# The second group's three fetched tiles: the scores go to DRAM, and their best 16 are searched in the dense pass

## The chip, the cores and the metric

The kernel runs on one core of one Trainium2 chip. The metric is the device time of one execution in microseconds. The engines are called PE (TensorE, matrix products), DVE (VectorE), ACT (ScalarE), POOL (GpSimd) and SP (SyncE, here only a queue of DMA issues). A line number such as L751 is a line of the kernel before.

## The reference, cut to what matters

One layer of a model: two mixers, then a channel mixer that looks up 16 of 16,384 single-neuron experts for each of 8 heads and each token. There are 9 tiles of 128 tokens. Of the channel mixer:

```python
def peer(x, w_q, sub_keys, u_tab, v_tab):
    q = (xt @ w_q).reshape(n_tok, PEER_HEADS, 2, PEER_QHALF)
    s = jnp.einsum('thpc,hpkc->thpk', q, sub_keys).astype(jnp.float32)
    v1, i1 = lax.top_k(s[:, :, 0], PEER_TOPK)
    v2, i2 = lax.top_k(s[:, :, 1], PEER_TOPK)
    cand = (v1[..., :, None] + v2[..., None, :]).reshape(n_tok, PEER_HEADS, PEER_TOPK * PEER_TOPK)
    ...
    top_v, top_j = lax.top_k(cand, PEER_TOPK)
    idx = jnp.take_along_axis(cand_idx, top_j, axis=-1)
    g = jax.nn.softmax(top_v, axis=-1)
    ...
        ue = jnp.take(u_tab, ib, axis=0)
        ve = jnp.take(v_tab, ib, axis=0)
        a = jax.nn.gelu(jnp.einsum('bd,bed->be', xb, ue)) * gb
        return jnp.einsum('be,bed->bd', a, ve)
```

So each token has 16 score vectors (8 heads, 2 halves) of 128 scores, and of each the best 16 values and their indices are needed. From these 32 the candidates of a head are formed, the best 16 of them chosen, and the experts' rows of two tables (1024 wide) used.

## The kernel before, in words

**Tiles and groups.** Tile 0 holds the context, tiles 1 to 8 the latent tokens. They pass through `group` as [0], then GA = [5,6,7,8], then GB = [1,2,3,4]. In the end the experts are computed in two ways. Tiles 0 to 3 (`GATHER`) are *fetched*: for each of 128 experts per token POOL fetches a row of 1024 with an indirect DMA (L802 from the first table, L815 from the second), DVE forms the dot product (L805) and, after the gelu, accumulates (L820); that is 256 row steps per tile. Tiles 5, 6, 7, 8 and 4 (`DENSE`) go through *all* experts, in a dense pass over 128 blocks e: a product with the first table (`hidden`, tile pH), the gelu (L988, tile a), DVE's multiplication with the weights in G (L1069), a split of the result in a high and a low half (ACT L99 for the high one, DVE L100 for the low one), and the product with the second table. Every matrix product here is made of three products of such halves (L129, L130, L131). The weights' tables are split in the same way as they arrive (uH/uL, vH/vL). Three of the five dense tiles keep their sums in PSUM (tile pout); the other two are "rotated": once in 4 blocks their products (tile prot) are added on DVE to accd (L1052).

**The query stage** of a group (end of `group`, from L738): 16 blocks b, each with a weight unit that is loaded and split (wH, wL), 24 matrix products into pq, a copy of them on ACT (qs, L748), the score products into one PSUM bank psc (one for each tile of the group, L751) and, for each tile, `top16` (L413 to L420) on DVE: MAX8, the index search, the replacement of the eight found, MAX8 and index search again. Values go to tv, indices to ti. For a dense tile `combine` follows (tile 4's in two halves, the first from block 8 on), with the indices turned into rt, and `build_G` forms G and writes it to DRAM (G_d), from where the dense pass reads it (tile Gt, L1061). For a fetched tile of GB, tv and ti are sent to DRAM (L760) and `combine` is left for later.

**The dense pass** does this later work: `combine_late` (L767) loads tv and ti of one tile (L780), runs `combine` in steps, and queues the tile's row steps. `fill`, called 16 times in 4 blocks (after each split and each rotated addition), issues 3 late steps for the first of the three tiles and 0.8 for the others (`LATE`), a later tile's from 60 row steps before the running tile's end (`LEAD`), and 1.525 row steps. While late work runs, the rows have the 4 buffers of one pool; otherwise 2 more, which are the ones that the late work uses. What late work issues on DVE passes through the helper `Paced`, so that the trace has it under one line, L119; row steps and late steps are held back by an order (not a wait) behind the last but one split.

All instructions' order on an engine is set by a scheduler from priorities and the data they need. SP issues nearly all loads and stores in program order of its own queue: a load that waits for its buffer holds back the ones behind it.

Of the kernel before, what the change touches and what calls it, by code (L numbers as in the profile page):

```python
# [9 lines left out]
F32 = mybir.dt.float32  # L10
# [10 lines left out]
NT = 9  # L21
# [30 lines left out]
def hybrid_kernel(ctx, tc, x_all, pos, c2t, w_ada, b_ada, wst, wspt, bsp, lbraw, vecs, fng, skt, state,  # L52
# [20 lines left out]
    o_d = dram.tile([NT, 128, 512], F32, name="o_d")  # L73
    tvi_d = dram.tile([NT, 128, 512], F32, name="tvi_d")
    h2r_d = dram.tile([NT, 128, D], F32, name="h2r_d")
# [486 lines left out]
    def group(gp, tiles, hpar, native):  # L562
# [164 lines left out]

        tv = [gp.tile([128, 8, 2, 16], F32, name="tv", bufs=n) for _ in range(n)]
        ti = [gp.tile([128, 8, 2, 16], U32, name="ti", bufs=n) for _ in range(n)]
        opd_q = lambda k: cut(h2, slice(None), k, slice(0, T))  # L730
        before = rate["gather"]
        rate["gather"] = before * RQ
        split_at = [i for i in range(n) if tiles is GB and tiles[i] in DENSE]
        halves = {}
        for b in range(16):
            if b == 8:
# [12 lines left out]
            pss = ptp("psc")  # L749
            for i in range(n):  # L750
                P.matmul(pss[:, i * 128:(i + 1) * 128], qs[:, i * 128:(i + 1) * 128], skb, start=True, stop=True)  # L751
            for i in range(n):
                top16(gp, pss[:, i * 128:(i + 1) * 128], tv[i][:, b // 2, b % 2, :], ti[i][:, b // 2, b % 2, :], 128)
        rate["gather"] = before
        for i in range(n):
            t = tiles[i]
            if tiles is GB and t in GATHER:

                for z, x in enumerate((tv[i], ti[i].bitcast(F32))):
                    nc.sync.dma_start(tvi_d[t][:, z * 256:(z + 1) * 256], x.rearrange("p a b c -> p (a b c)"))  # L760
                late.append(t)
            elif i in halves:
                choose_q.append(combine(gp, t, tv[i], ti[i], h0=4, res=halves[i]))
            else:
                choose_q.append(combine(gp, t, tv[i], ti[i]))

    def combine_late(t):  # L767
        cols = []

        def al(name, n, dt=F32):  # L770
            w = n if dt in (F32, U32) else (n + 1) // 2
            if not cols or cols[-1][1] + w > 1024:
# [6 lines left out]
        tvi = al("tvi", 512)  # L779
        nc.sync.dma_start(tvi, tvi_d[t])  # L780
        yield from combine(None, t, q(tvi[:, 0:256]), q(tvi[:, 256:512].bitcast(U32)), al,
                           lambda name: row(name).bitcast(F16), Paced())
# [223 lines left out]

    late_q = deque(combine_late(t) for t in late)
    C["coff"], C["clen"], C["cj"] = load_cs3(dp, row("cs32"))
# [185 lines left out]
```

## Time and profile before

| | us |
|---|---|
| median of 3 runs | 3658.97 (3655.87 to 3667.10) |
| the profiled execution | 3668.42 |
| its span in the trace | 3666.6 |
| query stage of GB (first to last score product) | 1558.69 to 1666.39 |
| first multiplication with G (the dense pass begins) | 1748.62 |
| late work of the second and of the third fetched tile begins | about 2237 and 2900 |
| last instruction on DVE | 3658.28 |

The profile's page shows PE busy in 91% of the span, DVE in 77%, ACT in 32% and POOL in 39%. In the dense pass a unit of four blocks takes 56.3 us where no late work runs (281.46 us for twenty blocks). An instruction's row in a timeline has start and duration in us, the engine, the line, the operation, out<-in; in brackets stands the idle time of its engine ahead of it and what ended it.

### The profile page before, as it was taken

To read this page: it belongs to the slowest core of one execution; us is meant where nothing else is said; L and a number is where in the kernel's file an instruction comes from. 1 tells how busy PE (TensorE), PEld (TensorE's weight loads), DVE (VectorE), ACT (ScalarE), POOL (GpSimd) and SP (SyncE) were. 2 spreads that over 40 slices of the span, in tenths; PEclk is the share of its full clock that TensorE was granted. 3 is DMA by queue.
4 is the path that set the end of the run, shared out by engine and by line. 5 is a ranking of instruction groups with operands and counts; after the bars stand their busy time and mean duration, and the time that the engine had idled before them with its cause. 6 is when DMAs were issued, how large, how long until landed. Compare 5 with 4: busy or idle time off the path is not lost. (4 is left out here: it accounts for less than half of the span.)

```text
span 3666.6 us, 48822 instructions
## 1 busy us (share of the span) xinstructions
PE 3343.5 (91%) x17547; PEld 2763.0 (75%) x17547; DVE 2841.6 (77%) x5427; ACT 1156.4 (32%) x2075; POOL 1436.9 (39%) x1128
## 2 busy tenths in 40 slices
PE   8888889898898899897899999989999989999997
PEld 4376778676576576576788888888898878898996
DVE  2317888787699986598787889887888888788888
ACT  2511334321323577726222222222222222222222
POOL 0002441454211220000265564655555456555654
PEclk9899999899999899897899999999999999999998
DMA  7787754688733676442898998898988799988986
GB/s 279 280 294 255 248 186 129 206 301 333 251 116 99 224 264 228 161 151 101 272 333 307 319 325 274 317 317 313 321 315 313 260 330 338 321 303 314 332 317 248
DMA packets 361956, 971.12 MB, mean 265 GB/s; under 512 B 32720, under 2 KB 142672, under 8 KB 356080
## 3 DMA queue, kind: packets, MB, share of 16 engines
q0 software_dynamic: 149824, 546.37, 42.3%
q1 hardware_dynamic: 211888, 421.62, 33.3%
q8 instruction: 138, 2.26, 0.2%
q14 instruction: 106, 0.87, 0.1%
HBM read 897.07 MB, written 70.80 MB: 264 GB/s over the span
## 5 line engine op out<-in xcount | busy, mean ns | idle before, releaser
L802 POOL DMA_INDIRECT gu<-in_urow_dram,ix x512 | 688.5, 1345 | 1003.7 <-DVE jk L805 374.1
L815 POOL DMA_INDIRECT gv<-in_vrow_dram,ix x512 | 694.9, 1357 | 736.4 <-DVE acc L820 399.9
L805 DVE SCALAR_TENSOR_TENSOR jk<-gu,h2r 128x1024 f16<-128x1024 f32 x512 | 625.6, 1222 | 139.9 <-DMA gu<-in_urow_dram,ix 124.8
L820 DVE SCALAR_TENSOR_TENSOR acc<-gv,act,acc 128x1024 f32<-128x1024 f32 x508 | 651.7, 1283 | 62.8 <-DMA gv<-in_vrow_dram,ix 53.3
L129 PE MATMUL pH<-h2DH,uH 128*128 128x320 f32 x2016 | 625.4, 310 | 12.9 <-DVE accd L1052 10.9
L131 PE MATMUL pH<-h2DH,uL 128*128 128x320 f32 x2016 | 622.9, 309 | 3.2 <-DVE uL L100 3.2
L130 PE MATMUL pH<-h2DL,uH 128*128 128x320 f32 x2016 | 623.4, 309 | 0.0
L129 PEld LDWEIGHTS pH<-h2DH,uH 128*128 128x128 f32 x2016 | 379.7, 188 | 23.0 <-DVE accd L1052 15.9
L130 PEld LDWEIGHTS pH<-h2DL,uH 128*128 128x128 f32 x2016 | 379.6, 188 | 4.4
L131 PEld LDWEIGHTS pH<-h2DH,uL 128*128 128x128 f32 x2016 | 379.4, 188 | 4.1 <-DVE uL L100 4.1
L129 PE MATMUL pout<-vH,aH 128*128 128x512 f32 x768 | 299.0, 394 | 23.0 <-ACT vH L99 16.3
L99 ACT ACTIVATE vH<-vr 128x1024 fp32r<-128x1024 f32 x128 | 133.4, 1058 | 568.9 <-DMA vr<-in_vrow_dram 294.3
L130 PE MATMUL pout<-vL,aH 128*128 128x512 f32 x768 | 302.0, 393 | 5.0 <-DVE vL L100 5.0
L131 PE MATMUL pout<-vH,aL 128*128 128x512 f32 x768 | 302.0, 393 | 2.1 <-DVE aL L100 2.1
L129 PE MATMUL prot<-vH,aH 128*128 128x512 f32 x512 | 211.7, 414 | 56.9 <-DVE accd L1052 50.8
L99 ACT ACTIVATE wH<-wraw 128x1024 fp32r<-128x1024 f32 x118 | 124.9, 1060 | 437.9 <-PE pq L130 145.2
L100 DVE TENSOR_TENSOR vL<-vr,vH 128x1024 fp32r<-128x1024 f32 x128 | 156.3, 1221 | 86.9 <-ACT vH L99 84.5
L130 PE MATMUL prot<-vL,aH 128*128 128x512 f32 x512 | 208.4, 407 | 0.0
L99 ACT ACTIVATE uH<-ur 128x1024 fp32r<-128x1024 f32 x126 | 133.3, 1058 | 237.1 <-PE pH L130 197.5
L131 PE MATMUL prot<-vH,aL 128*128 128x512 f32 x512 | 207.7, 406 | 0.0
L99 ACT ACTIVATE aH<-a 128x640 fp32r<-128x640 f32 x128 | 94.2, 736 | 357.1 <-DVE a L1069 284.2
L550 PEld LDWEIGHTS <-oh 128*128 128x128 f16 x1280 | 130.5, 120 | 80.7 <-issue 65.0
(343 smaller groups left out, 6442.7 us busy)
## 6 DMA issues: line engine op xcount, KB each, us to landing
wraw<-in_wst_dram SPq DMA_DIRECT2D x216, 512.0 KB
vr<-in_vrow_dram SPq DMA_DIRECT2D x128, 512.0 KB
ur<-in_ut_dram SPq DMA_DIRECT2D x126, 512.0 KB
G_d<-Gs SPq DMA_DIRECT2D x40, 1024.0 KB
Gt<-G_d SPq DMA_DIRECT2D x160, 256.0 KB
wraw<-in_w_ada_dram SPq DMA_DIRECT2D x48, 512.0 KB
gu<-in_urow_dram,ix POOLq DMA_INDIRECT x512
gv<-in_vrow_dram,ix POOLq DMA_INDIRECT x512
```

Of the source, the lines that this page charges most:

```text
L99: A.activation(H, src, AF.Copy)
L100: return V.tensor_tensor(out=L, in0=src, in1=H.bitcast(F32), op=OP.subtract)
L129: P.matmul(ps, a[0], b[0], start=first, stop=False)
L130: P.matmul(ps, a[0], b[1], start=False, stop=False)
L131: P.matmul(ps, a[1], b[0], start=False, stop=last)
L550: P.matmul(pg[:, tt * 128:(tt + 1) * 128], oh[:, 0, :, tt], og[a][:, :, tt], start=(a == 0), stop=(a == 1))
L802: G.indirect_dma_start(out=ur, out_offset=None, in_=urow, in_offset=bass.IndirectOffsetOnAxis(ap=ix[:, c:c + 1], axis=0))
L805: paced(V.scalar_tensor_tensor(jk, ur, 1.0, h2r, op0=OP.mult, op1=OP.mult, accum_out=dots[:, k:k + 1]))
L815: G.indirect_dma_start(out=vr, out_offset=None, in_=vrow, in_offset=bass.IndirectOffsetOnAxis(ap=ix[:, c:c + 1], axis=0))
L820: paced(V.scalar_tensor_tensor(acc, vr, act[:, k:k + 1], acc, op0=OP.mult, op1=OP.add))
```

## The change: what it does

In the query stage of GB only tile 4 is still searched. The scores of tiles 1 to 3 (384 columns of the PSUM bank) are copied by ACT into a buffer sw and sent by SP to DRAM (sc_d), once a block; the score product of tile 4 is put ahead of the other three. tv and ti no longer go to DRAM. In the dense pass `combine_late` loads a tile's scores in two loads of 512 KB into two row buffers (packets of 512 bytes) and searches them, 16 searches in 8 further steps, before the steps it had. From there on, nothing is changed; 12 lines are added, so that L1069 becomes L1081, L1061 becomes L1073, L805 becomes L817 and so on.

```diff
-    tvi_d = dram.tile([NT, 128, 512], F32, name="tvi_d")
+    sc_d = dram.tile([16, 128, 3 * 128], F32, name="sc_d")
...
+        wait = [i for i in range(n) if tiles is GB and tiles[i] in GATHER]
+        now = [i for i in range(n) if i not in wait]
...
             pss = ptp("psc")
-            for i in range(n):
+            for i in now + wait:
                 P.matmul(pss[:, i * 128:(i + 1) * 128], qs[:, i * 128:(i + 1) * 128], skb, start=True, stop=True)
-            for i in range(n):
+            if wait:
+                w0, m = wait[0], len(wait) * 128
+                sw = h512("sw")
+                A.activation(sw[:, :m], pss[:, w0 * 128:w0 * 128 + m], AF.Copy)
+                nc.sync.dma_start(sc_d[b], sw[:, :m])
+            for i in now:
                 top16(gp, pss[:, i * 128:(i + 1) * 128], tv[i][:, b // 2, b % 2, :], ti[i][:, b // 2, b % 2, :], 128)
...
-                for z, x in enumerate((tv[i], ti[i].bitcast(F32))):
-                    nc.sync.dma_start(tvi_d[t][:, z * 256:(z + 1) * 256], x.rearrange("p a b c -> p (a b c)"))
-                late.append(t)
+                late.append((t, wait.index(i)))
...
-        nc.sync.dma_start(tvi, tvi_d[t])
-        yield from combine(None, t, q(tvi[:, 0:256]), q(tvi[:, 256:512].bitcast(U32)), al,
+        tv, ti = q(tvi[:, 0:256]), q(tvi[:, 256:512].bitcast(U32))
+        for z in range(2):
+            sc = row("sc").rearrange("p (b j) -> p b j", b=8)
+            nc.sync.dma_start(sc, sc_d[z * 8:z * 8 + 8, :, w * 128:(w + 1) * 128].rearrange("b p j -> p b j"))
+            for b in range(8):
+                top16(None, sc[:, b, :], tv[:, z * 4 + b // 2, b % 2, :], ti[:, z * 4 + b // 2, b % 2, :], 128, Paced())
+                if b % 2:
+                    yield
+        yield from combine(None, t, tv, ti, al,
                            lambda name: row(name).bitcast(F16), Paced())
```

What this does to the order of instructions is seen at three places. **On DVE in the query stage**, a part of the searches that stand between two splits of weight units (wL) in a block before:

```order
L100 TENSOR_TENSOR wL<-wraw,wH 128x1024
L419 MAX tv<-mrep 128x8
L415 MAX tv<-psc 128x8
L420 MAX_INDEX ti<-tv,mrep 128x8
L416 MAX_INDEX ti<-tv,psc 128x8
L418 MATCH_REPLACE mrep<-tv,psc 128x128
L415 MAX tv<-psc 128x8
L419 MAX tv<-mrep 128x8
L416 MAX_INDEX ti<-tv,psc 128x8
L420 MAX_INDEX ti<-tv,mrep 128x8
L418 MATCH_REPLACE mrep<-tv,psc 128x128
```

and now the whole of what stands between two such splits:

```order
L100 TENSOR_TENSOR wL<-wraw,wH 128x1024
L415 MAX tv<-psc 128x8
L416 MAX_INDEX ti<-tv,psc 128x8
L418 MATCH_REPLACE mrep<-tv,psc 128x128
L419 MAX tv<-mrep 128x8
L420 MAX_INDEX ti<-tv,mrep 128x8
L100 TENSOR_TENSOR wL<-wraw,wH 128x1024
```

Four searches in a block have become one, and none of the three others is left in this stage.

**On DVE at the start of the dense pass**, from the last work on the G matrices (L533) over the cast of a table of constants (L873) to the first multiplications with Gt; before:

```order
L533 TENSOR_TENSOR oh<-oh,gl 128x512
L873 CAST cs_13760<-cs_13759 128x768
L1069 TENSOR_TENSOR a_13010<-a_13010,Gt 128x640
L1069 TENSOR_TENSOR a_13069<-a_13069,Gt 128x640
L119 TENSOR_TENSOR late<-late 128x8x16
L100 TENSOR_TENSOR aL<-a_13010,aH 128x640
```

and now (late is where the late work keeps its values, sc a tile's scores; the cast is L885, the multiplication L1081):

```order
L119 MAX_INDEX late<-late,sc 128x8 x2
L119 MATCH_REPLACE sc<-late,sc 128x128 x2
L119 MAX late<-sc 128x8 x2
L119 MAX_INDEX late<-late,sc 128x8 x2
L119 MAX late<-sc 128x8 x2
L119 MAX_INDEX late<-late,sc 128x8 x2
L119 MATCH_REPLACE sc<-late,sc 128x128 x2
L119 MAX late<-sc 128x8
L1081 TENSOR_TENSOR a_12758<-a_12758,Gt 128x640
L119 MAX_INDEX late<-late,sc 128x8
L119 MAX late<-sc 128x8
L1081 TENSOR_TENSOR a_12817<-a_12817,Gt 128x640
```

Between the cast and the first multiplication there stand now some five and a half searches of the first fetched tile, of which the piece shows the last rows (the first row of sc comes right behind the cast); the other ten and a half come behind the multiplication, between the splits of the first blocks.

**On SP's queue** where the second fetched tile's late work begins, with the loads of the dense pass around it (ur, vr: the two tables; Gt: the weights); before:

```order
L1061 DMA Gt<-G_d 128x4x128 x4
L1029 DMA vr<-in_vrow_dram 128x1024 [waits DMAHW3_49,DVE_49]
L780 DMA late<-tvi_d 128x512 [waits DMASW3_49,DMASW4_49,DMASW2_49,DMASW6_49,DMASW1_49,DMAHW4_49,DMASW0_49,DVE_49]
L1029 DMA ur<-in_ut_dram 128x1024 [waits DMAHW5_49,DVE_49]
L1029 DMA vr<-in_vrow_dram 128x1024 [waits DMAHW6_49,DMAHW3_49,DVE_49]
```

and now:

```order
L1041 DMA ur<-in_ut_dram 128x1024 [waits DMAHW7_49,DVE_49]
L1041 DMA vr<-in_vrow_dram 128x1024 [waits DMAHW6_49,DMAHW0_49,DVE_49]
L788 DMA sc<-sc_d 128x8x128 [waits DMASW3_49,DMASW4_49,DMASW2_49,DMASW6_49,DMASW1_49,DMAHW1_49,DMASW0_49,DVE_49]
L1041 DMA ur<-in_ut_dram 128x1024 [waits DMAHW2_49,DVE_49,Activation_49]
L788 DMA sc<-sc_d 128x8x128 [waits DMASW5_49,DMASW7_49,DMASW3_49,DMAHW3_49,DMASW1_49,DVE_49]
L1041 DMA vr<-in_vrow_dram 128x1024 [waits DMAHW4_49,DMAHW7_49,DVE_49,Activation_49]
```

The one load of 256 KB has become two of 512 KB with one load of ur between them, and each waits for its row buffer (the semaphores named DMASW are POOL's fetches, which used that buffer). The load of vr ahead of the first of them waits for DVE. On DVE itself the first search of these scores stands directly behind a split of ur, the one that sets this vr's buffer free:

```order
L100 TENSOR_TENSOR aL<-a,aH 128x640
L832 SCALAR_TENSOR_TENSOR acc<-gv,act,acc 128x1024
L817 SCALAR_TENSOR_TENSOR jk,dots<-gu,h2r 128x1024
L832 SCALAR_TENSOR_TENSOR acc<-gv,act,acc 128x1024
L100 TENSOR_TENSOR uL<-ur,uH 128x1024
L119 MAX late<-sc 128x8 x2
L119 MAX_INDEX late<-late,sc 128x8 x2
L119 MATCH_REPLACE sc<-late,sc 128x128 x2
```

Before, a split of vr and a dot product stood ahead of the first late instruction at that place, and those values were a quarter as large.

## Rows read from the trace of the kernel before

**Rows 1.** The page: the span, and its first part, busy time of each engine, share of the span and instructions.
```profile
span 3666.6 us, 48822 instructions
PE 3343.5 (91%) x17547; PEld 2763.0 (75%) x17547; DVE 2841.6 (77%) x5427; ACT 1156.4 (32%) x2075; POOL 1436.9 (39%) x1128
```

**Rows 2.** Busy time by stretch (start:end and length in us; then the busy time of PE, of its weight loads, of DVE, ACT and POOL with the number of instructions, TensorE's granted clock as a share of full speed, the busy share of the DMA engines, GB/s). The first stretch is the second group's query stage, the second the build of its G matrices; the others lie in the dense pass, and begin where DVE starts to multiply the first of four blocks by G: twenty blocks without late work, the four blocks in which the second gathered tile's late work runs, the four blocks behind them, the twenty blocks that begin with that late work, and the twelve that begin with the third tile's.
```profile
1560.00:1670.00 110.00, 99.54 (x484) 80.86 (x483) 106.35 (x578) 26.00 (x33) 1.18 (x2) 0.95 0.36 125
1687.00:1737.00 50.00, 33.40 (x256) 28.36 (x256) 38.98 (x85) 47.31 (x128) 0.00 (x0) 0.50 0.31 127
1955.47:2236.93 281.46, 279.01 (x1559) 253.84 (x1558) 238.71 (x290) 71.02 (x104) 165.39 (x120) 0.99 0.91 318
2236.93:2315.19 78.26, 66.87 (x354) 59.80 (x353) 67.78 (x157) 17.36 (x24) 35.67 (x27) 0.91 0.73 239
2315.19:2371.70 56.51, 55.56 (x306) 49.15 (x305) 46.95 (x63) 15.16 (x22) 34.40 (x25) 1.00 0.99 367
2236.93:2555.70 318.77, 293.88 (x1607) 264.19 (x1606) 262.33 (x389) 76.16 (x110) 175.71 (x127) 0.96 0.87 304
2900.07:3088.84 188.77, 173.06 (x930) 154.23 (x929) 161.39 (x203) 46.80 (x68) 110.39 (x81) 0.96 0.92 325
```

**Rows 3.** The instructions that touch the tile tv, all of the kernel's searches in the query stages: how many, shortest/median/longest in ns, first and last start. One search is one of each kind shown here, and a second index search on mrep like the first on psc.
```profile
L415 DVE MAX8 tv<-psc x144: 277/290/304, 265.5 to 1670.8; 128x8 f32<-128x128 f32 x144
L416 DVE FIND_INDEX8 ti<-tv,psc x144: 281/290/306, 266.0 to 1671.3; 128x8 uint32<-128x128 f32 x144
L418 DVE MATCH_REPLACE8 mrep<-tv,psc x144: 272/280/299, 266.3 to 1671.8; 128x128 f32<-128x128 f32 x144
L419 DVE MAX8 tv<-mrep x144: 269/277/305, 266.7 to 1672.2; 128x8 f32<-128x128 f32 x144
```

**Rows 4.** The timeline of DVE in one block of the query stage (start and duration in us): successive searches' first instructions, and the split of the next weight unit.
```profile
1560.69 0.29 DVE L415 MAX8 tv<-psc 128x8 f32<-128x128 f32 x1
...
1561.87 0.29 DVE L415 MAX8 tv<-psc 128x8 f32<-128x128 f32 x1
...
1563.05 0.29 DVE L415 MAX8 tv<-psc 128x8 f32<-128x128 f32 x1
...
1564.24 1.22 DVE L100 TENSOR_TENSOR wL<-wraw,wH 128x1024 fp32r<-128x1024 f32 x1
```

**Rows 5.** The timeline of PE in the query stage: the score products of the first block, of the second and the third, the longest wait (in brackets the idle time ahead of an instruction and what ended it), and the score products of the sixteenth block.
```profile
1558.69 1.09 PE L751 MATMUL psc<-skb,qs 128*128 128x128 f32 x8
...
1563.59 1.09 PE L751 MATMUL psc<-skb,qs 128*128 128x128 f32 x8
...
1570.12 1.09 PE L751 MATMUL psc<-skb,qs 128*128 128x128 f32 x8
...
1625.56 0.80 PE L131 MATMUL pq<-h2H,wL 128*128 128x512 f32 x1 [8.62 <-DVE wL L100]
...
1666.39 1.16 PE L751 MATMUL psc<-skb,qs 128*128 128x128 f32 x8 [1.40 <-ACT qs L748]
```

**Rows 6.** The timeline of ACT at the same place: an exponential of tile 4's softmax.
```profile
1627.34 0.26 ACT L488 ACTIVATE ex<-ex 128x64 f32<-128x64 f32 x1 [10.31 <-DVE ex L487]
```

**Rows 7.** The timeline of DVE from the last block of the query stage to the first multiplication by G: the sixteenth block's first and fourth search, the cast that opens the build of the G matrices, the last work of that build, and the multiplication.
```profile
1667.59 0.30 DVE L415 MAX8 tv<-psc 128x8 f32<-128x128 f32 x1 [0.20 <-PE psc L751]
...
1670.83 0.29 DVE L415 MAX8 tv<-psc 128x8 f32<-128x128 f32 x1
...
1686.65 0.42 DVE L507 CAST rt<-pidx 128x256 f16<-128x256 f32 x1 [0.70 <-PE pidx L505]
...
1733.24 0.55 DVE L873 CAST cs<-cs 128x768 f16<-128x768 f32 x1
1748.62 1.56 DVE L1069 TENSOR_TENSOR a<-a,Gt 128x640 f32<-128x640 f32 x2 [14.84 <-DMA Gt<-G_d]
```

**Rows 8.** The timeline of PE at the start of the dense pass: the two waits for DVE there.
```profile
1756.50 0.50 PE L130 MATMUL pout<-vL,aH 128*128 128x512 f32 x1 [1.08 <-DVE vL L100]
...
1762.94 0.42 PE L131 MATMUL pH<-h2DH,uL 128*128 128x320 f32 x1 [1.73 <-DVE uL L100]
```

**Rows 9.** The waits in the four blocks of the second tile's late work: engine, tile and line, what it waited for, us in total, how many, the longest.
```profile
POOL gu L802 <- DVE late L119: 12.8, 4, 8.2
...
PE pH L129 <- DVE accd L1052: 6.9, 1, 6.9
...
DVE acc L820 <- DMA gv<-in_vrow_dram,ix: 6.2, 5, 2.4
...
PE prot L129 <- DVE accd L1052: 4.5, 1, 4.5
...
DVE jk L805 <- DMA gu<-in_urow_dram,ix: 4.2, 2, 3.8
```

**Rows 10.** The timeline of all engines in the dense pass: the issue of a load of 512 KB on SP's queue, and ACT's first use of it.
```profile
1772.64 0.33 SPq L1029 DMA_DIRECT2D vr<-in_vrow_dram  x1
...
1776.07 1.06 ACT L99 ACTIVATE vH<-vr 128x1024 fp32r<-128x1024 f32 x1 [3.77 <-DMA vr<-in_vrow_dram]
```

**Rows 11.** The timeline of DVE at the end of the program: the last accumulation of gathered rows, the last addition of a rotated tile's product, and the last instruction.
```profile
3630.65 1.27 DVE L820 SCALAR_TENSOR_TENSOR acc<-gv,act,acc 128x1024 f32<-128x1024 f32 x1
...
3644.82 0.68 DVE L1052 TENSOR_TENSOR accd<-accd,prot 128x512 f32<-128x512 f32 x1
...
3658.28 1.29 DVE L840 SCALAR_TENSOR_TENSOR accd<-accd,rstd,fgd 128x1024 f32<-128x1024 f32 x1 [0.72 <-POOL rstd L95]
```

More of the change, by code (lines that the diff above doesn't have):

```diff
@@ L726, in group @@
                                           h2[z].a[kh][:, :, i * 128:(i + 1) * 128].bitcast(F32))
-        tv = [gp.tile([128, 8, 2, 16], F32, name="tv", bufs=n) for _ in range(n)]
-        ti = [gp.tile([128, 8, 2, 16], U32, name="ti", bufs=n) for _ in range(n)]
+        late_of = [t for t in tiles if tiles is GB and t in GATHER]
+        tv = [t not in late_of and gp.tile([128, 8, 2, 16], F32, name="tv", bufs=n) for t in tiles]
+        ti = [t not in late_of and gp.tile([128, 8, 2, 16], U32, name="ti", bufs=n) for t in tiles]
         opd_q = lambda k: cut(h2, slice(None), k, slice(0, T))
@@ L765, in group, with combine_late @@
                 choose_q.append(combine(gp, t, tv[i], ti[i]))
-    def combine_late(t):
+    def combine_late(t, w):
         cols = []
@@ L1005, in hybrid_kernel @@
     vt = vrow.rearrange("(e p) d -> e p d", p=128)
-    late_q = deque(combine_late(t) for t in late)
+    late_q = deque(combine_late(*x) for x in late)
     C["coff"], C["clen"], C["cj"] = load_cs3(dp, row("cs32"))
```

## The prediction

> **What bounds the kernel now.** I read the page first: PE is busy in 91% of the span of 3666.6 us, DVE in 77% [rows 1]. That is an average over stages with different limits, so I read the busy time by stretch next [rows 2]. In the dense pass without late work PE is busy in 279.01 of 281.46 us, and DVE in 238.71: 56.3 us for four blocks, of which DVE works 47.7 and has 8.6 us to spare. In the query stage both are near full: of 110 us PE has 99.54 and DVE 106.35. The build of G behind it is ACT's (47.31 of 50 us). Then I read what the late work costs today. The four blocks that hold the second tile's take 78.26 us, where PE is busy only 66.87, its clock is at 0.91 and DVE works 67.78. The four blocks behind them are normal again (56.51 us). In their waits PE stands twice for DVE's additions to accd, 6.9 and 4.5 us; POOL's fetches wait 12.8 us for late work to leave its buffers, and DVE waits 6.2 and 4.2 us for fetched rows [rows 9]. So DVE is short in the query stage, has some 15% to spare in the steady dense pass, and is the engine that sets the pace in the late windows. The change takes DVE work from the first place and puts it in the third.
>
> **What is moved.** A search is five instructions of 277 to 290 ns and their value loads [rows 3]; successive searches start 1.18 us apart, and three of them take 3.55 us up to the split behind them [rows 4]. I take 1.19 us: 16 searches of a tile are 19 us, all 48 are 57 us. In the dense pass the same instructions read SBUF; the row on mrep, which lies there, has 277 ns where the one on psc has 290, so I leave the price as it is.
> [...]
>
> **The query stage: -9.7 us.** Undisturbed blocks follow each other in 6.53 us, which is PE's own work (1563.59 to 1570.12). From the first score product to the sixteenth there are 107.70 us, and 15 intervals are 97.95. The rest is nearly one event: PE waits 8.62 us for a split wL on DVE [rows 5], because ACT, in order, stands 10.31 us behind an exponential whose input DVE delivers late, behind searches [rows 6]. With one search in four left, DVE has some 57 us more to spare there, and PE sets the pace. Nothing below PE's 6.53 us can be won. The added copy sw on ACT (one in a block; ACT works 26.00 of 110 us) and one store of 192 KB on SP a block lie beside it. Bounds: 0 if ACT's stall stays as it is, -10.4 if every wait in rows 5 goes.
>
> **Behind the stage: -3.2 us.** Tile 4's last search begins at 1670.83, as the fourth of its block; the first began at 1667.59 [rows 7]. Searched first, tile 4 is 3.24 us earlier, and its combine, ACT's build of G and the load of Gt move forward with it as a chain. Bounds: 0 to -3.2. So the dense pass begins 12.9 us earlier.
>
> **The first tile's 19 us: +7.** DVE has nothing to do for 14.84 us ahead of the first multiplication [rows 7]. The order puts 5.5 searches there, 6.5 us, which that idle time hides. The other 10.5, 12.5 us, come behind the multiplication, between the splits on which PE starts. Before, PE waited there only 1.08 and 1.73 us for DVE [rows 8], so there is little cover. All of these searches stand in the order ahead of the first split of ur, where today a part of the older late steps stands, which moves behind it. I take +7, a little over half, with 0 and 12.5 as bounds.
>
> **The two later windows: 2 x 19 = +38.** This is the term that decides. At 0.8 steps for each of 16 fills in four blocks, 8 more steps make a window 10 fills longer, 12.5 becomes 22.5. What does a us of DVE's work cost in such a window? The second tile's first four blocks have 78.26 - 56.3 = 21.96 us more time with 67.78 - 47.7 = 20.04 us more work: 1.10. The third tile's twelve blocks: 188.77 less 3 x 56.3 is 19.9 us, with 161.39 less 3 x 47.7, 18.3 us: 1.09. Taken over twenty blocks it is 37.31 us for 23.62 us: 1.58 [rows 2]. So the spare 8.6 us in four blocks have not paid for the late work today. Against that, the longer window brings ten more fills with their own slack, 10/16 x 8.6 = 5.4 us: 19 x 1.10 - 5.4 = 15.5 us. For more, DVE's waits for fetched rows (10.4 us in that window [rows 9]), as the rows have four buffers for ten fills longer. I take 1.0, 19 us in each window; bounds 0 (all slack used) and 30 (1.58).
>
> **The load at the second tile's start: +4.** SP issues the load of the scores behind a load of vr, which waits for the same split that stands directly ahead of the first search on DVE. So DVE must wait out a transfer of 512 KB, and everything in order behind the search waits too: the multiplication by Gt, the splits, the additions to accd. Such a load was used 3.4 us after its issue [rows 10]. Before the third tile there are some 7 us of row steps between; I put nothing there. I take 4; bounds 0 (PE has work ahead) and 6.9 (two loads).
>
> **The end: +4.5.** The fetched row steps finish later against the dense pass: by the order four more accumulations and the fetched tile's final work come behind the last additions to accd, where before the last accumulation (3630.65) lay well ahead of them (3644.82) [rows 11]. Four of 1.27 us and three instructions of about 1.22 us are 8.8 us; DVE had small idle gaps there (0.72 us ahead of the last row). I take half; bounds 0 and 8.8.
>
> **Sum.** -12.9 + 7 + 38 + 4 + 4.5 = +40.6 us on the profiled execution's 3668.4, so 3709. That execution lies 9.45 us above the median of 3658.97, so against the median I predict 3700. With all lower bounds it is -13.6, or 3645; with all upper ones +88, or 3747.
>
> **Rivals.**
> *The slack takes it all.* DVE is 85% busy in the steady dense pass; if its 8.6 us in four blocks absorb the 19 us over two or three units and the additions to accd are not late, the windows and the load cost nothing. Then -12.9 and 0 to +7 at the start and 0 to 4 at the end: 3646 to 3657, say 3651. For it: the searches come spread, 2.4 us a step, where the old steps have instructions up to 2.3 us and fetches that wait for buffers. Against it: 1.09 and 1.10 in rows 2, with the same slack. It decides from the point where DVE has worked off what a unit of four blocks brings, with its 8.6 us, before PE needs accd again.
> [...]
> [...]
> *The query stage gains nothing.* The copy sw stands on ACT in order ahead of the next wH, and the store on SP among the weight loads; if they hold up the splits, 9.7 us are not won: 3710. Against it: ACT's 26.00 us.
> *Half is absorbed.* Each window costs 9 us: 3680.
>
> **How the numbers follow.** A measurement of this kernel tells some 0.3%, or 11 us, from no change: faster is below 3648, slower above 3670. Chances: forecast (3688 to 3715) 0.49; half absorbed (3670 to 3688) 0.13, of which 0.02 falls within 0.3%; all absorbed 0.18, half of it faster and half within; costlier windows 0.10; no gain in the query stage 0.10. So faster 0.09, within 0.11, slower 0.80. The range is 3653 to 3729: it leaves out a part of the absorbed case below and of the costlier one above.
>
> **What would show it.** Right: score products 6.53 us apart throughout, no wait for wL; first multiplication with Gt near 1736; DVE almost without idle time in the units that hold the second and third tiles' searches, these units together some 40 us longer, PE waiting for accd there; a DVE wait for sc at the second tile's start; gathered rows ending behind the last rotated addition. Wrong: those units near 56 us each with the searches inside, or DVE idle while PE waits for something else there; then my price of a us of late work is the step that failed.

## The result, and the profile after

The changed kernel takes 3700.97 us (median of 4 runs, 3695.65 to 3703.28), the kernel before 3663.03 in the same comparison. The ratio is 1.0103, with a 95% interval of 1.008 to 1.0126: 1.0% slower, 38 us. Forecast were 3700 us and +41 us. The changed kernel's page:

```profile
span 3698.2 us, 48846 instructions
PE 3354.6 (91%) x17547; PEld 2767.1 (75%) x17547; DVE 2841.6 (77%) x5427; ACT 1165.1 (32%) x2091; POOL 1446.2 (39%) x1128
```

DVE's total is the same to the tenth as before [rows 1], 2841.6 us: the searches were moved, and not one us of work was saved or added. So none of the 38 us is DVE's work. PE's busy time is up by 11.1 us for the same 17,547 products; the rest is waiting.

To find it, the dense pass is cut at the same blocks e in every kernel, where DVE starts the multiplication with G (read from DVE's timeline of L1069, or what that line became). Blocks 28 to 48 hold the second fetched tile's late work, 76 to 92 the third's; the last column goes from block 124 to the end of the span. "Before, again" is the kernel before profiled once more (first experiment below). "Front" is the time from the query stage's first score product to the first multiplication.

| us | front | 0-16 | 16-28 | 28-48 | 48-76 | 76-92 | 92-124 | 124-end | whole pass |
|---|---|---|---|---|---|---|---|---|---|
| before | 189.9 | 240.3 | 171.7 | 308.5 | 405.8 | 247.4 | 461.3 | 83.1 | 1918.0 |
| before, again | 190.2 | 239.9 | 171.5 | 307.3 | 402.3 | 248.5 | 458.7 | 83.5 | 1911.7 |
| changed | 181.1 | 238.3 | 170.3 | 332.0 | 400.4 | 275.6 | 460.3 | 91.7 | 1968.7 |

The front is 8.9 us shorter (forecast 12.9), the pass 53.8 us longer than the mean of the two rows of before (forecast 53.5). Together that is +45; the two profiled executions differ by less, since the program up to the query stage, where nothing is changed, took 10.3 us less in the one after (first score product at 1548.4, before at 1558.7).

These are the rows behind the long stretches, busy time by stretch with the columns of [rows 2], in the changed kernel (blocks 0 to 16, 28 to 48, 76 to 92, 124 to the end):

```profile
1729.53:1967.84 238.31, 215.04 (x1144) 193.89 (x1145) 203.87 (x398) 61.00 (x86) 119.80 (x88) 0.93 0.83 291
2138.16:2470.20 332.04, 295.52 (x1574) 262.35 (x1573) 279.48 (x524) 74.98 (x109) 167.88 (x124) 0.95 0.85 289
2870.59:3146.23 275.64, 241.44 (x1250) 213.19 (x1250) 230.27 (x463) 61.35 (x88) 137.37 (x100) 0.93 0.82 280
3606.51:3698.20 91.69, 60.93 (x320) 53.72 (x318) 70.63 (x81) 16.32 (x27) 37.99 (x34) 0.85 0.68 244
```

and the same blocks of the kernel before, profiled again:

```profile
1733.60:1973.50 239.90, 213.38 (x1145) 191.74 (x1145) 195.63 (x317) 61.12 (x86) 118.79 (x92) 0.94 0.88 303
2145.03:2452.35 307.32, 285.60 (x1558) 256.79 (x1557) 262.03 (x397) 74.97 (x109) 169.14 (x124) 0.96 0.88 308
2854.64:3103.11 248.47, 232.14 (x1256) 205.71 (x1255) 213.47 (x338) 60.82 (x88) 137.48 (x101) 0.98 0.88 308
3561.76:3645.30 83.54, 60.57 (x318) 53.42 (x316) 65.72 (x73) 16.49 (x27) 31.65 (x30) 0.88 0.67 241
```

In the second and third row DVE has 17.5 and 16.8 us more work, and the stretch is 24.7 and 27.2 us longer: more than the work that was added. DVE is not full there either, 279 of 332 us. Unit by unit, the searches of the second tile stand in blocks 32 to 40 and the rest of its late work reaches to 44; the third tile's searches stand in 76 to 80, the rest reaches to 84. In these five units of four blocks DVE idles 9.6, 6.3, 10.1, 4.9 and 18.4 us, where a steady unit has 8.6:

```profile
2197.79:2264.08 66.29, 62.53 (x341) 55.85 (x340) 56.65 (x148) 13.93 (x20) 29.00 (x20) 1.00 0.77 257
2264.08:2333.51 69.43, 57.46 (x292) 49.37 (x290) 63.12 (x174) 14.14 (x21) 27.26 (x21) 0.93 0.74 236
2333.51:2405.91 72.40, 62.13 (x328) 54.96 (x327) 62.30 (x83) 17.30 (x25) 43.26 (x31) 0.93 0.88 308
2870.59:2938.46 67.87, 58.69 (x310) 52.04 (x310) 62.97 (x215) 13.48 (x20) 30.14 (x22) 0.95 0.80 261
2938.46:3020.81 82.35, 66.28 (x333) 57.25 (x333) 63.94 (x130) 18.31 (x24) 34.82 (x25) 0.92 0.71 240
```

So something beside the work costs. The waits in blocks 28 to 48 of the changed kernel name two kinds of it, as [rows 9] did before:

```profile
PE pout L130 <- DVE vL L100: 17.2, 3, 9.6
PE prot L129 <- DVE accd L1064: 11.2, 4, 5.4
...
DVE jk L817 <- DMA gu<-in_urow_dram,ix: 18.5, 10, 4.9
...
DVE acc L832 <- DMA gv<-in_vrow_dram,ix: 5.8, 3, 3.8
DVE late L119 <- DMA sc<-sc_d: 3.6, 2, 3.2
...
POOL gv L827 <- DVE late L119: 18.6, 9, 9.4
```

PE waits for DVE; but DVE itself waits 24.3 us for fetched rows (15.2 in the kernel before, again), and POOL's fetches wait for late work to give up its buffers.

Counted on PE, the 24.7 us are 15.0 us more waiting (36.5 beside 21.5) and 9.9 us more busy time (295.52 beside 285.60). In blocks 76 to 92 the 27.2 us are 18.1 us more waiting (34.0 beside 15.9) and 9.3 us more busy time (241.44 beside 232.14). There the waits for ACT grew most, in the changed kernel

```profile
PE prot L129 <- ACT a L1000: 6.8, 1, 6.8
PE pout L129 <- ACT aH L99: 5.1, 2, 4.5
```

and in the kernel before, again (the first line is of blocks 76 to 92; the other two are all of PE's waits in 28 to 48):

```profile
PE prot L129 <- ACT a L988: 0.7, 1, 0.7
...
PE prot L129 <- DVE accd L1052: 14.8, 3, 9.0
PE pH L129 <- DVE accd L1052: 6.7, 1, 6.7
```

The number of recorded products is nearly the same (1574 and 1558, 1250 and 1256), and the granted clock was 0.95 and 0.93 where it had been 0.96 and 0.98. So some 19 of the 52 us are, as the profile counts busy time, slower products (188 beside 183 ns of busy time for each recorded one, and 193 beside 185) and not waiting. No run here holds the clock, so how much of this would remain without the waits is open.

The places that the prediction named, first on PE's timeline (query stage, and the first split of ur in the pass, [rows 5, 8] before), then on DVE's (start of the pass, the second tile's first search, and the end, [rows 7, 11] before):

```profile
1559.85 1.09 PE L754 MATMUL psc<-skb,qs 128*128 128x128 f32 x8
1569.85 1.13 PE L754 MATMUL psc<-skb,qs 128*128 128x128 f32 x8 [3.31 <-DMA skb<-in_skt_dram]
...
1748.31 0.63 PE L131 MATMUL pH<-h2DH,uL 128*128 128x320 f32 x1 [6.78 <-DVE uL L100]
```

```profile
1714.08 0.48 DVE L119 MAX8 late<-sc 128x8 f32<-128x128 f32 x2
...
1716.43 0.47 DVE L119 MAX8 late<-sc 128x8 f32<-128x128 f32 x2
...
1729.53 0.83 DVE L1081 TENSOR_TENSOR a<-a,Gt 128x640 f32<-128x640 f32 x1 [9.07 <-DMA Gt<-G_d]
...
2235.04 0.49 DVE L119 MAX8 late<-sc 128x8 f32<-128x128 f32 x2 [3.18 <-DMA sc<-sc_d]
...
3667.48 0.69 DVE L1064 TENSOR_TENSOR accd<-accd,prot 128x512 f32<-128x512 f32 x1
3668.08 1.28 DVE L832 SCALAR_TENSOR_TENSOR acc<-gv,act,acc 128x1024 f32<-128x1024 f32 x1
...
3689.87 1.28 DVE L852 SCALAR_TENSOR_TENSOR acc<-acc,rstd,fg 128x1024 f32<-128x1024 f32 x1 [0.72 <-POOL rstd L95]
```

The wait for DVE in the query stage (8.62 us before) is gone; a wait for a load of sub-keys (skb) has come in its place. Two searches follow two in 2.35 us. The load of the second tile's scores keeps DVE 3.18 us, and the last accumulation now lies behind the last rotated addition.

### The profile page after: what moved, and what is told of

It is laid out like the page before. It is cut to its first block, busy times and chain, and to the rows that moved or that the text cites. A ratio compares the mean times of both kernels' runs of the same rounds, so it can differ in the third digit from the quotient of the medians.

```text
span 3698.2 us, 48846 instructions
## 1 busy us (share of the span) xinstructions
PE 3354.6 (91%) x17547; PEld 2767.1 (75%) x17547; DVE 2841.6 (77%) x5427; ACT 1165.1 (32%) x2091; POOL 1446.2 (39%) x1128
## 5 line engine op out<-in xcount | busy, mean ns | idle before, releaser
L817 DVE SCALAR_TENSOR_TENSOR jk<-gu,h2r 128x1024 f16<-128x1024 f32 x512 | 625.3, 1221 | 140.6 <-DMA gu<-in_urow_dram,ix 134.3
L129 PEld LDWEIGHTS pout<-vH,aH 128*128 128x128 f32 x768 | 147.0, 192 | 57.9 <-ACT vH L99 16.4
```

Of the source, the lines that this page charges most:

```text
L129: P.matmul(ps, a[0], b[0], start=first, stop=False)
L817: paced(V.scalar_tensor_tensor(jk, ur, 1.0, h2r, op0=OP.mult, op1=OP.mult, accum_out=dots[:, k:k + 1]))
```

## The experiments

My theory was that the whole loss sits in the two later windows and at the end, that a us of late DVE work costs a us because DVE has no room in a short window, and that the query stage's gain is real. The rivals: any search in the dense pass costs its time, wherever it stands; or it is not DVE's work but the length of the window, in which the fetched rows have four buffers in place of six. All comparisons are against the kernel before on the same chip. The stretches that the readings rest on:

| us | front | 0-16 | 28-48 | 48-76 | 76-92 | 124-end | whole pass |
|---|---|---|---|---|---|---|---|
| only the first tile late | 184.4 | 240.2 | 307.9 | 396.6 | 255.3 | 91.1 | 1917.3 |
| before, loads and steps only | 190.4 | 227.4 | 316.2 | 399.5 | 263.6 | 90.4 | 1927.9 |
| before, searched twice | 192.7 | 237.3 | 328.4 | 399.9 | 277.2 | 90.9 | 1965.5 |
| changed, spread thin | 179.5 | 239.2 | 337.2 | 439.1 | 267.2 | 91.0 | 2030.3 |
| before, four row buffers | 189.9 | 247.2 | 327.1 | 434.7 | 277.7 | 87.1 | 2057.1 |
| changed, scores apart | 181.3 | 246.3 | 331.1 | 400.7 | 273.0 | 90.4 | 1979.2 |
| changed, three sub-key buffers | 176.3 | 238.2 | 331.5 | 399.8 | 276.3 | 90.4 | 1965.2 |
| changed, windows as long as before | 179.5 | 251.3 | 327.1 | 407.5 | 265.4 | 84.2 | 1962.4 |
| before, only longer windows | 190.5 | 239.9 | 316.4 | 404.1 | 250.9 | 83.2 | 1924.5 |
| first tile late, three sub-key buffers | 179.2 | 234.2 | 310.4 | 395.6 | 255.7 | 91.6 | 1914.3 |
| the same, fetches denser | 179.2 | 234.1 | 319.3 | 401.0 | 257.7 | 82.8 | 1929.8 |

**The kernel before, again.** No edit.

> The kernel before, unchanged, profiled a second time, to see which of its stretches belong to the one execution that was shown. If the units that looked long there without late work (65.0 us from the third unit of four blocks on, 1866.1 to 1931.1) are the kernel's, they come again; if they were that execution's, the unit has 55 to 58 us, and the dense pass up to the fifth unit is some 8 us shorter against its start.

It took 3647.07 us in its one execution. The pass differs by 6 us from the first profile's, the unit asked for was 64.3 us long again, so it is the kernel's own; the time up to the first score product differs by 15.3 us (1543.4 and 1558.7) with identical code. So a profiled execution's total says little about 10 us of change, and the stretches within the pass, or the medians, must be compared.

**Only the first tile late.** Its edit in the changed kernel:

```diff
-        late_of = [t for t in tiles if tiles is GB and t in GATHER]
+        late_of = [t for t in tiles if tiles is GB and t == 1]
...
-        wait = [i for i in range(n) if tiles is GB and tiles[i] in GATHER]
+        wait = [i for i in range(n) if tiles[i] in late_of]
         now = [i for i in range(n) if i not in wait]
+        if tiles is GB:
+            now = now[::-1]
...
+        if w is None:
+            nc.sync.dma_start(tvi, tvi_d[t])
```

> Only tile 1 (the first fetched tile of the second group) is searched in the dense pass; tiles 2 and 3 are searched in the query stage as before and go to DRAM as values and indices. Theory (what was added in the two later windows is the whole loss): these windows fall back to their length of before, the query stage and the chain behind it keep some 6 to 9 us of gain, the first tile's searches cost nothing in the end; time 6 to 12 us under the kernel before, some 3652. Rival (any search in the dense pass costs its full 19 us): 8 to 13 us above the kernel before, some 3674.

Measured 3660.38, ratio 0.9995 (0.9982 to 1.0008): between the two. The loss of the windows is gone (the pass has 1917.3 us), so the later two tiles are the loss, as the theory says; but the front gained only 5.6 us, less than I took, and the pass gave nothing back. The lines with `now` keep tile 4's search ahead of the others, as in the changed kernel. The trace shows the same wait for skb as the changed kernel, 3.66 us. It also shows what a later start of the fetches does: 48-76 is 7.5 us shorter and 76-92 7.3 us longer than before though no late work was added there. So for kernels whose fetches start later, this row, not the kernel before, is what windows are compared with.

**The kernel before with loads and steps only.**

```diff
         nc.sync.dma_start(tvi, tvi_d[t])
+        for z in range(2):
+            sc = row("sc")
+            nc.sync.dma_start(sc, x1_d[t])
+            for b in range(4):
+                Paced().tensor_copy(sc[:, b * 8:b * 8 + 4], sc[:, b * 8 + 4:b * 8 + 8])
+                yield
```

The loads bring other data (x1_d), in rows of 1024 values in place of 128.

> The kernel before, with the two loads of 512 KB and the 8 further steps in each late window, but no search in them: four copies of 4 columns each on each load, 0.07 us or so apiece. Theory (the cost of the windows is DVE's work): at most 4 us a window, mainly the wait for the load, time 0 to 10 us above the kernel before. Rival (the cost is the longer time in which the fetched rows have only four buffers, and the loads): about 20 us a window, 40 us above the kernel before.

Measured 3672.48, ratio 1.0035 (1.002 to 1.005), +10.5 us: just over the theory's upper edge, far from the rival in the total. By stretches it is no small thing: against the row above, 28 to 92 is 19.5 us longer (8.3, 2.9 and 8.3) without one search, in part hidden in the total by a shorter start (0-16).

**The kernel before, searched twice.** The same edit with the 16 searches on other data in place of the copies:

```diff
+            for b in range(8):
+                o = 768 + b * 16
+                top16(None, sc[:, b % 6 * 128:b % 6 * 128 + 128], sc[:, o:o + 16], sc[:, o + 128:o + 144].bitcast(U32), 128, Paced())
+                if b % 2:
+                    yield
```

> The kernel before, with the loads and the 16 searches of a late tile made in addition in each late window, on other data, their results unused; the query stage is as before. Theory: the dense pass loses what it lost in the changed kernel, 23 to 28 us in each of the two later windows and 8 us at the end, so 50 to 60 us above the kernel before, and the difference to the changed kernel, 10 to 19 us, is what the query stage and its chain gained. Rival (the windows got longer for another reason, such as the freed query stage shifting the fetches against the dense pass): less than 30 us above the kernel before.

Measured 3716.63, ratio 1.0148 (1.0117 to 1.0179), +55 us: the theory. Its windows are those of the changed kernel, with the query stage untouched; so the loss is made in the dense pass alone. The difference between this kernel and the one above is the price of the searches themselves. The rows of blocks 28 to 48 and 76 to 92, loads and steps only:

```profile
2143.16:2459.40 316.24, 290.40 (x1570) 260.49 (x1569) 261.00 (x404) 74.53 (x109) 171.05 (x124) 0.96 0.86 303
2858.94:3122.57 263.63, 234.91 (x1258) 209.62 (x1257) 213.61 (x343) 60.24 (x88) 135.84 (x100) 0.95 0.85 295
```

and searched twice:

```profile
2157.55:2485.99 328.44, 295.09 (x1560) 262.95 (x1559) 278.84 (x525) 75.22 (x109) 170.09 (x124) 0.94 0.84 292
2885.89:3163.14 277.25, 238.06 (x1250) 211.03 (x1249) 230.33 (x464) 61.22 (x88) 138.19 (x100) 0.94 0.81 279
```

34.6 us more DVE work make 25.8 us more time: 0.75 us a us, not 1.0. By this, a quarter of the searches goes into DVE's slack. In blocks 0 to 16 the two kernels differ by 9.9 us: the first tile's searches cost there too.

**The changed kernel, spread thin.**

```diff
-LATE = (3, 0.8)
-LEAD = 60
+LATE = (3, 0.2)
+LEAD = 150
```

> The changed kernel with the late steps of the second and third tile four times as thin (0.2 steps a fill in place of 0.8, begun 150 row steps before the running tile's end in place of 60). By count DVE then has 2.98 + 0.2 x 2.4 = 3.46 us a fill of its 3.52. Theory (a late us costs a us because DVE is overfull in a short window): the 19 us of searches of each tile, and part of the older 22 us, go into DVE's slack; time 30 to 60 us under the changed kernel, so at or under the kernel before. Rival (the cost comes from the four row buffers while late work runs, so from the window's length): time 20 us or more above the changed kernel.

Measured 3768.20, ratio 1.029 (1.0263 to 1.0316): 67 us above the changed kernel. My theory fell here, and the rival's number was passed. In blocks 28 to 48 this kernel has DVE work like the kernel before (262.15 us beside 262.03) and takes 30 us more:

```profile
2171.80:2509.03 337.23, 289.53 (x1541) 257.86 (x1542) 262.15 (x392) 73.70 (x109) 170.50 (x126) 0.93 0.81 280
```

What DVE does meanwhile is in its waits in that stretch: 58.2 us for fetched rows, where the kernel before, again, has 10.6 and 4.6:

```profile
DVE jk L817 <- DMA gu<-in_urow_dram,ix: 36.5, 19, 3.8
DVE acc L832 <- DMA gv<-in_vrow_dram,ix: 21.7, 21, 3.0
```

The added work is not what starves PE there; the fetch stream is held up as long as late work runs.

**The kernel before with four row buffers throughout.**

```diff
-        rows_of[:] = [(gat, NGR)] * NGR + [(dp, NGD)] * (0 if busy else NGD)
+        rows_of[:] = [(gat, NGR)] * NGR + [(dp, NGD)] * 0
```

> The kernel before with four row buffers for the fetched rows through the whole dense pass (before: six, and four only while late work runs). Theory (in a late window the fetches are short of buffers, which costs some 0.5 us a fill, as the thin spread showed): some 400 fills more at four buffers, 100 to 200 us above the kernel before. Rival (four are enough; what costs in the thin spread are the buffers that the scores take out of these four): under 20 us above it.

Measured 3803.80, ratio 1.0398 (1.0372 to 1.0425), +143 us: the theory. Blocks 16 to 28 have no late work in either kernel, and DVE has 144.27 us of work in them, before 144.03. With four buffers:

```profile
1988.00:2176.12 188.12, 176.90 (x967) 158.59 (x966) 144.27 (x169) 42.44 (x62) 98.54 (x74) 0.98 0.88 299
```

with these waits of DVE,

```profile
DVE jk L805 <- DMA gu<-in_urow_dram,ix: 16.2, 9, 3.9
DVE acc L820 <- DMA gv<-in_vrow_dram,ix: 12.1, 9, 2.3
```

and with six (the kernel before, again):

```profile
1973.50:2145.03 171.53, 169.48 (x944) 152.93 (x943) 144.03 (x170) 42.54 (x62) 98.85 (x73) 1.00 0.91 316
```

with this one:

```profile
DVE jk L805 <- DMA gu<-in_urow_dram,ix: 7.6, 3, 2.9
```

16.6 us in 48 fills are 0.35 us a fill. The changed kernel's two windows are ten fills longer each: 20 x 0.35 is 7 us, an estimate.

**The changed kernel with the scores apart.** Eight loads of 128 KB into two halves of the late work's own buffers, one step ahead, in place of two row buffers:

```diff
-            sc = row("sc").rearrange("p (b j) -> p b j", b=8)
...
+        two = [al("sc", 256).rearrange("p (b j) -> p b j", b=2) for _ in range(2)]
...
+        fetch(0)
+        for h in range(8):
+            if h < 7:
+                fetch(h + 1)
+            for b in range(2):
+                top16(None, two[h % 2][:, b, :], tv[:, h, b, :], ti[:, h, b, :], 128, Paced())
+            yield
```

> The changed kernel, but the scores of a late tile do not go into two of the row buffers: they come in eight loads of 128 KB into two halves in the late work's own buffers, each load one step ahead of its search. The fetched rows keep all four buffers while the searches run. Theory (a part of a window's cost is the row buffer that the scores hold for four steps, and the first search's wait for its load): 10 to 20 us under the changed kernel. Rival (the cost is DVE's searches alone): within 6 us of the changed kernel.

Measured 3709.16, ratio 1.0128 (1.0105 to 1.015): 8 us above the changed kernel, so the theory fell. DVE's waits for the scores fell only from 4.4 to 3.6 us, and 28 to 92 is 3.2 us shorter than in the changed kernel; but the start of the pass is 8.0 us longer. The trace shows why: ahead of the first multiplication DVE now waits 15.49 us for Gt without any search, where the changed kernel has 6.38 us of searches and a wait of 9.07 us; these searches now come behind the multiplication:

```profile
1728.96 0.83 DVE L1085 TENSOR_TENSOR a<-a,Gt 128x640 f32<-128x640 f32 x1 [15.49 <-DMA Gt<-G_d]
```

The row buffer that the scores hold is not what the windows cost.

**The changed kernel with three buffers for the sub-keys.**

```diff
-            skb = gp.tile([128, 128], F32, name="skb", bufs=2)
+            skb = gp.tile([128, 128], F32, name="skb", bufs=3)
```

> The changed kernel with three buffers for the sub-keys (skb) in place of two. Theory (the store of the scores on SP and its transfer make one load of sub-keys 3.3 us late, which is what the query stage fell short of the forecast): no wait of PE for skb, the query stage 98 us from first to last score product in place of 101, time 3 us under the changed kernel, which is at the limit of what can be measured; the trace decides. Rival (another load is late instead): PE waits as long for a weight unit.

Measured 3689.61, ratio 1.0083 (1.0058 to 1.0109). PE has no wait for skb left, the stage runs from 1546.7 to 1644.6 (97.9 us; changed 102.3, before 108.6), and the front is 4.8 us shorter than the changed kernel's. The median lies 11 us under the changed kernel's, and the ratios 0.2% or 7 us apart; 3.5 us of it the trace places in the pass. I had expected 3.

**The changed kernel with windows as long as before.**

```diff
-LATE = (3, 0.8)
+LATE = (5.4, 1.44)
```

> The changed kernel, with late steps 1.8 times as dense (5.4 a fill for the first tile, 1.44 for the others, before 3 and 0.8), so that its 18 steps take as many fills as the 10 steps of the kernel before. Theory (two parts: the searches' DVE work, some 25 us, and the window's ten fills more, some 20 us, and the fetch stream's later start, 8 us at the end): the end falls back to its length of before, the later windows lose 10 to 20 us, time 15 to 25 us under the changed kernel. Rival (DVE's total work in the windows is all that counts, and bunching it makes PE's waits worse): no difference or slower than the changed kernel.

Measured 3699.84, ratio 1.0109 (1.0094 to 1.0125): no difference, the rival's number. By stretches both happened: 28 to 92 are 40 us longer than in the kernel before (changed: 48 against the row with only the first tile late), and the end is at its length of before, 84.2 us; but the first 16 blocks, where the first tile's 18 steps are now packed as tightly, are 13 us longer than the changed kernel's. What is won at the end and in the windows is paid at the start.

**The kernel before with longer windows only.**

```diff
-LATE = (3, 0.8)
+LATE = (3, 0.445)
```

> The kernel before, with its 10 late steps of the second and third tile thinned to 0.445 a fill, so that they take the 22.5 fills of the changed kernel's 18; no search, no load, no row buffer more. Theory (length alone costs): 10 to 25 us above the kernel before, as the loads-only kernel's two later windows, which were 24 us longer. Rival (there the loads and the row buffers that they held were the cost, or the steps' positions): within 6 us of the kernel before.

Measured 3673.60, ratio 1.0038 (1.0024 to 1.0053), +13 us: the theory, at its lower end. The windows are 8.5 and 2.9 us longer, without any work more. So of the 19.5 us of the loads-only kernel some 11 are length (the rate of the kernel with four row buffers gives 7). The split is rough: the profiled execution was the fastest of nine, 11 us below their median.

**The first tile late, with three buffers for the sub-keys.** The edits of the second and of the eighth experiment together.

> Only the first fetched tile's searches in the dense pass, as in the first experiment, and three buffers for the sub-keys. Theory: the query stage's 3.7 us wait for a load of sub-keys goes; 3 to 6 us under the first experiment, 4 to 9 us under the kernel before, some 0.2%. Rival (the first tile's searches cost as much as the query stage gains, whatever the loads do): within 3 us of the kernel before.

Measured 3647.26, ratio 0.9964 (0.995 to 0.9977): 0.36% faster than the kernel before, and so the fastest of all. Its query stage runs from 1552.0 to 1650.3, 98.3 us, without a wait of PE for DVE or for skb, though DVE still makes three of the four searches of every block there; the pass is that of the kernel before, 1914.3 us. The gain of 13 us is more than the 4 to 9 that I expected. Around the place of the old stall DVE is busy all the time, 30.00 of 30 us, and PE in 29.45 of them:

```profile
1603.00:1633.00 30.00, 29.45 (x145) 23.56 (x144) 30.00 (x154) 9.12 (x15) 0.00 (x0) 1.00 0.32 103
```

So it may be that searching tile 4 first, and not the room on DVE, ended the stall. The kernel before with tile 4 first and nothing moved was not run; this stays open.

**The same, with denser fetches.**

```diff
-RATE = (4, 2.6, 0.5, 2.5, 6.1, 4.5)
+RATE = (4, 2.6, 0.5, 2.5, 6.15, 4.5)
```

> The kernel with only the first fetched tile's searches in the dense pass and three buffers for the sub-keys, with the fetches issued 0.8% more densely (6.15 in place of 6.1). Theory (the 8 us at the end come because the fetched rows start some four row steps late and so end behind the last rotated additions): the last accumulation lies ahead of these again, the stretch from the last unit to the end has 83 us in place of 91, time 4 to 8 us under that kernel, 15 to 20 us under the kernel before. Rival (what stands at the end is only moved: denser fetches cost DVE in the pass what the end gains): within 3 us of that kernel.

Measured 3664.35, ratio 1.0014 (1.0003 to 1.0026). The end is repaired as the theory says (82.8 us): it is long where the fetched rows end late. But the pass is 15.5 us longer, 8.9 of it in blocks 28 to 48 and 10.6 in 92 to 124 (467.2 beside 456.6), and the kernel is 17 us slower. The rival had the trade right and its price too low: it had put the time within 3 us.

## Why the prediction was right, step by step

The sum was right to a few us; two terms were right for the reason given, and others were off in ways that cancelled: the front gained 4 us less, the first tile and the end cost 5 us less, the windows and the load 6 us more. That these cancel is luck.

- *The searches' price, 1.19 us:* 1.18 us in the late work (2.35 for two). MAX8 on the scores in SBUF has a median of 278 ns there, on psc 290 [rows 3]: 12 ns apart, beside the 13 of mrep and psc by which I had left the price as it was.
- *The query stage, -9.7:* -6.3 (102.3 against 108.6 us). The 8.62 us wait is gone, as forecast; whether the room on DVE or the new order of the searches did it is open (above). The miss is a wait that I did not see: one load of sub-keys came 3.3 us late. With a third buffer the stage is at -10.7, a little past my bound. I had written the store of the scores down as lying beside ACT's and SP's other work, and it shares SP's queue with this load; but that the store made it late is not shown. No run leaves the store alone out, and the kernel before, again, which has no store, waits 0.6 us for the same load.
- *Behind the stage, -3.2:* -2.5.
- *The first tile, +7, and the end, +4.5:* the two belong together, which I had not seen. At the first split of ur PE does wait 6.78 us. But with 8 more steps at 3 a fill the fetches start 2.7 fills later; that unloads the start and is paid at the end. The start has -1.8, the end +8.4, together 6.6 where I had 11.5; with the steps packed so that the fetches start as before, it is +11.2 and +0.9.
- *The two windows, +38, and the load, +4:* 48.2 between blocks 28 and 92, against the kernel with only the first tile late. The load's wait is 3.2 us, as forecast. The price of 1.0 was the sum of two things that I had as bounds on either side: the searches themselves cost 0.75 us a us, 26 us, since the slack takes a quarter; and the windows' length costs some 11 us, 7 of them by the rate of the kernel with four row buffers, where DVE waits 28.3 us for fetched rows in blocks 16 to 28 (7.6 with six). I had named these waits, and gave them no term of their own, only the step from 15.5 to 19 us a window. The remaining 8 us of the loads-only kernel's 19.5 go with its loads and steps; the scores' row buffers are not their cause, and I leave them open.
- *The third tile's row.* Its late work began at 2877 us in the kernel before, not at about 2900, so the row that gave 1.09 leaves out the first 23 us of that stretch. Blocks 76 to 88, which hold all of it, have 23.0 us more time than 3 x 56.3 and 23.2 us more work than 3 x 47.7, a price of 0.99:

```profile
2874.90:3066.80 191.90, 178.15 (x958) 158.04 (x957) 166.35 (x284) 46.47 (x67) 103.80 (x77) 0.97 0.87 303
```

- *The signs.* PE waits for accd, DVE for sc, and the gathered rows end last, as forecast. But DVE is not almost without idle time: it comes near that where the searches stand (4.9 us idle in blocks 76 to 80), and behind them, in blocks 80 to 84, it idles 18.4 us, while PE waits 11.5 us for ACT. The prediction had named DVE idle while PE waits for something else as the sign that its price of a us of late work had failed. The price came near in size, but not in what it is made of.
- *The rivals.* The slack that takes all is refuted by the kernel searched twice. Costlier windows, at the price of 1.58 that is the windows' upper bound and leads to the 3729 at the end of the range, were nearer than I thought: 48 us for 38 us of work is 1.27, and spread thin it is far above it, 84 us or 2.2. What part the granted clock has in this no run isolates: it was 0.95 and 0.93 in the windows, 0.96 and 0.98 before, with some 19 us more busy time of PE.

## What to carry to other kernels

Moving work off a crowded stage pays only as far as the wait that bounds the stage: here the stall was gone with one of three tiles moved and tile 4 searched first, and the other two tiles, once moved, cost more than 40 us in a stage that looked 15% idle. When work is put into a background window, price the window as well as the work: what it holds while it is open (here two of six row buffers, 0.35 us a fill) is lost for its whole length, so thinning it out can cost more than crowding it (here 67 us more; crowding it made no difference). And when a stage is tightened or given a store, check the loads that come just in time: here one buffer more for the sub-keys removed a wait of 3.3 us.

## What the runs showed that was not expected

Identical code reached its query stage at 1543.4 us in one execution and at 1558.7 in another, with the same pass behind it to 6 us. Fetches issued 0.8% more densely made the pass 15.5 us longer, though the fetched rows are the same and DVE's work differs by 1 us (2634 and 2633 us from 460 us to the end, added up from its timelines). I read this as a fetch stream at the edge of what DVE can take; no run shows it by itself.
